# Stores, loads and the start of attention in a hybrid encoder block: three-dimensional query and key stores, whole loads issued early, and a merge that adds in PSUM

## The chip, the core and the metric

The kernel runs on one core of one Trainium2 chip. Its time is the device time of one execution in microseconds (us); three runs of the kernel before took 1420.76, 1419.35 and 1420.70, median 1420.7. TensorE (PE; its weight loads are PEld), VectorE (DVE), ScalarE (ACT), GpSimd (POOL) and SyncE (SP, which only issues DMA here) each run their own instructions in order and wait for each other by semaphores.

## The reference, cut to what matters

One layer of an encoder over 1024 tokens with a width of 1024. Two branches read the same RMS-normalized input through one projection: dilated window attention (three groups of eight heads of 64) and a gated linear recurrence. The part that the change touches is the way of the queries and keys:

```python
for g, (window, dilation) in enumerate(((128, 1), (512, 4), (2048, 16))):
    q = rms_norm(qkv_a[:, :, g, 0], q_norm_w[layer, g])   # over each head's 64 channels
    k = rms_norm(qkv_a[:, :, g, 1], k_norm_w[layer, g])
    v = qkv_a[:, :, g, 2]
    o_g, m_g, d_g = dilated_window_attention(q, k, v, ...)  # keys gathered by residue mod dilation
...
wts = jnp.stack(dens) * jnp.exp(m_all - jnp.max(m_all, axis=0, keepdims=True))
o_a = jnp.sum(wts[..., None] * jnp.stack(outs), axis=0) / jnp.sum(wts, axis=0)[..., None]
y_a = (o_a * silu(g_a)) @ w_proj_a
```

Everything is float32. The kernel splits each operand of a large product into a high and a low part and adds three products.

## The kernel before, in words

**How it is ordered.** A planner in Python (classes Plan and Builder) writes the instructions out once, when the kernel is built. It keeps an estimated time for every engine and every tile. Work is queued as tasks with a priority (a smaller number goes first), the tiles it depends on and, where needed, a condition that a buffer is about to be free. After each few matmuls `tick` issues the tasks whose time by the estimates has come; `burst` does the same for small products on TensorE. `quiet` says whether only weight splits and weight loads are left, and `drain` waits for that. What is issued runs on the chip in that order on each engine, behind semaphores, whatever the real times are. All engine instructions pass through one helper, which is why the profile shows line L60 for all of them; the names of the tiles tell them apart.

**The stages.** The input is normalized and the values are projected (to about 142 us); 27 blocks project queries and keys, gates and others (to 669 us); the products called gp project more columns, with attention between and beside them (to about 845); the three groups are merged (to 915); the recurrence follows (to 1222); then come the output projections (to the end).

**The blocks** (`run_quads`). Each block does seven products out of sums of the input (tiles S0 to S3, each with a high and a low part, 64 KB a partition in all) and of the weights (`qraw`, its differences formed on DVE, its high parts on ACT as `whi`, its low parts on GpSimd or DVE as `wlo`). Twelve of the blocks are queries and keys: group g, side hv (four heads), e (0 for queries, 1 for keys). Each gives two halves of the tokens, and each half has two tiles of 128 partitions, one per value of col, which hold 32 of the 64 channels of each of four heads. They pass through this chain, one task after another: `squares` (ACT, takes two buffers of the ring `ny`, which has four), `sq_sum` (DVE), `sq_high` (ACT), `sq_low` (DVE), `head_sums` (TensorE: two products with ones, tile `nss`), `guess` (ACT, takes three buffers of `ny`), `newton` and `norm_root` (DVE), `scaled` (DVE, once per col), and the store `out` by SP to the DRAM tensor qkD[g, hv, 2e + col], 128 rows (head by head, 32 channels each) of 1024 tokens. There are 48 such stores of 256 KB. Their pieces are 2 KB (group 0, and the keys of group 2), 512 bytes (group 1) or 128 bytes (queries of group 2), because tokens are sorted by residue. A buffer of `ny` is free again when its store has landed.

**Attention's start.** After the blocks, `for pr in range(2)` runs eight gp groups a turn. After the first of them `attention_start` drains the tasks, closes the blocks' pools and that of the sums, opens the rooms for attention and queues the four loads of `h10D` (`back_load`, split by `back_split`; needed before the fifth gp group), and for every (g, hv), beginning with group 2, the loads of keys `ak`, queries `aq`, biases `abias` and eight of values `av`. `load_heads` loads a tile of two heads' halves by four DMAs of 32 partitions with 2 x 4 KB each, since partition 64 j + 32 col + c has to hold channel half col of heads j and 2 + j. The scores (`sc`) are TensorE products of keys and queries, and DVE adds the biases when it reads them.

**The merge.** `merge_maybe` opens the merge's room, and `spread_al` spreads the weights of the three groups over PSUM (three tiles `al`) and has DVE multiply and add: near = al0 x og0, acc = al1 x og1, far = al2 x og2, near + far, acc + near, acc x gate. While it runs, the low parts of the gp weights are made on the engine that `b.low` names: DVE.

Of the kernel before, what the change touches and what calls it, by code (L numbers as in the profile page):

```python
# [9 lines left out]
F32R = mybir.dt.float32r  # L10
# [3 lines left out]
OP = mybir.AluOpType  # L14
# [4 lines left out]
S = 1024  # L19
# [15 lines left out]
VR, PT = 10, 8  # L35
# [200 lines left out]
class Builder:  # L236
# [85 lines left out]
        self.p.t["pe"] = self.p.given  # L322

    def quiet(self):
        return all(t.fn in (self.split_next_page, self.feed) for t in self.tasks)

    def ring(self, pool, tag, bufs, shape, dtype=F32):
        return Ring(self, pool, tag, bufs, shape, dtype)
# [234 lines left out]
class Ring:  # L563
# [30 lines left out]
    def soon(self, n=1):  # L594
        return self.room(n) and self.when(n) <= self.b.p.t["pe"] + self.b.AHEAD
# [60 lines left out]
def hybrid_block(ctx, tc, a, out):  # L656
    b = Builder(ctx, tc, a)
    a_, v_, g_, t_, s_ = b.p.act, b.p.dve, b.p.pool, b.p.pe, b.p.sp
# [15 lines left out]
    hctx = ExitStack()  # L674
# [3 lines left out]
    def bank(name):  # L678
        t = b.bank.get(name=name)
        b.bank.done(t)  # L680
        return t

    stage = b.ring(stg, "stage", 3, [128, 512])
# [71 lines left out]
    hq = [{}, {}]  # L755
    for t in range(2):
        for k in range(2):
            for e in range(2):
                pool = a21pool if (t, k) == (1, 0) else hpool
# [9 lines left out]
    actx = ExitStack()  # L769
# [12 lines left out]
    acc = [v_ring.get() for _ in range(2)]  # L782
# [109 lines left out]
    qkD = dr.tile([3, 2, 4, 128, S], F32, name="qkD")  # L892
# [127 lines left out]
    def root(k):  # L1020
        rs[k] = inv_rms(k, bank("ss"))
        rs["d", k] = spread(rs[k])

    def root_out(k):
        rs["B", k] = spread_out(rs["d", k])
# [20 lines left out]
    at = {0: {11: lambda: root(1)}, 3: {5: lambda: root_out(1), 11: lambda: root(0)}, 7: {5: lambda: root_out(0)}}  # L1046
# [46 lines left out]
    gctx, sctx, tctx = ExitStack(), ExitStack(), ExitStack()  # L1093
    blk = {"n": 0}
# [150 lines left out]
    def scaled(g, hv, e, half, z, y2, o, col, count):  # L1245
        R = RES[g]
        n = 512 // R
        per = lambda t: t.rearrange("p (r u) -> p r u", r=R) if R > 1 else t
        nat = lambda t: t.rearrange("p (u r) -> p r u", r=R) if R > 1 else t
        v_.tensor_tensor(per(o), nat(y2), nat(z), op=OP.mult)  # L1250
        (b.rawr if id(z) in lent else blk["spare"]).done(z)
        count[0] -= 1
        if count[0] == 0:
            blk["y"].done(y2)

        def out():
            to = qkD[g, hv, 2 * e + col]
            if g == 2 and e == 1:
                s_.dma_start(to[:, 512 * half:512 * half + 512], o)
            else:  # L1260
                s_.dma_start(to.rearrange("p (r u) -> p r u", r=R)[:, :, n * half:n * half + n],
                             o.rearrange("p (r u) -> p r u", r=R))
            blk["y"].done(o)
        b.task("sp", [o], out, 1)
# [33 lines left out]

    att = {}

    def attention_start(now=False):
        if att or not (now or (not b.small and b.quiet())):
            return
        b.drain()
        gctx.close()
        sctx.close()
        p = hctx.enter_context(tc.tile_pool(name="h10b", bufs=1, side="right"))
        psum(2)
        b.eager, b.SLACK = True, 0.25
        ap = actx.enter_context(tc.tile_pool(name="attn", bufs=1))  # L1310
        for n, k, shape in (("v", VR, [128, 256]), ("q", 2, [128, 2, S]), ("k", 2, [128, 2, S]),
                            ("s", 6, [128, 3, 4, 64]), ("pt", PT, [128, 2, 2, 128]), ("os", 2, [128, 2, 2, 128]),
                            ("bias", 2, [128, 4, 256])):
            att[n] = b.ring(ap, "a" + n, k, shape)
        for e in range(2):
            hq[e][1, 0] = p.tile([128, 4, 512], F32R, name=f"hb{'hl'[e]}")
        for c in range(4):
            b.task("sp", [], lambda c=c: back_load(c), 1, stage.soon)
        for o, g in enumerate((2, 1, 0)):
            for hv in range(2):  # L1320
                soon = lambda n, k=2 * o + hv: att[n].soon() and (k == 0 or b.wire(3.5))
                for n, f in (("k", load_k), ("q", load_q), ("bias", load_bias)):
                    b.task("sp", [], lambda g=g, hv=hv, f=f: f(g, hv), 2, lambda n=n, soon=soon: soon(n))
                for i in range(8):
                    b.task("sp", [], lambda g=g, hv=hv, i=i: load_v(g, hv, i), 2, lambda soon=soon: soon("v"))

    def back_load(c):
        t = stage.get()
        s_.dma_start(t, h10D[c])
        b.task("act", [t], lambda: back_split(c, t), 2)  # L1330

    def back_split(c, back):
        hi, lo = hq[0][1, 0][:, c], hq[1][1, 0][:, c]
        a_.activation(hi, back, AF.Copy)
        v_.tensor_tensor(lo, back, hi.bitcast(F32), op=OP.subtract)
        stage.done(back)
        att["h"] = att.get("h", 0) + 1

    QT, KT, BIAS, V, left = {}, {}, {}, {}, {"in": 0, "out": 0, "turned": 0}

    def load_heads(t, at):
        for j in range(2):
            for col in range(2):
                s_.dma_start(t[64 * j + 32 * col:64 * j + 32 * col + 32],
                             at[col].rearrange("(p j c) t -> j c p t", p=2, j=2)[j])

    def load_k(g, hv):
        KT[g, hv] = att["k"].get()
        load_heads(KT[g, hv], qkD[g, hv, 2:4])
        score_tasks(g, hv)  # L1350

    def load_q(g, hv):
        QT[g, hv] = att["q"].get()
        load_heads(QT[g, hv], qkD[g, hv, 0:2])
        score_tasks(g, hv)

    def load_v(g, hv, i):
# [239 lines left out]
    def merge_maybe(now=False):  # L1597
        if mer or not (now or len(stored) == 48) or not att:
            return
        if now:  # L1600
            b.drain()
        b.eager, b.SLACK = False, 0.6
        b.low = "dve"
        psum(3)
        actx.close()
        mer["p"] = mctx.enter_context(tc.tile_pool(name="merge", bufs=1, side="right"))
        mer["sel"] = sel = mer["p"].tile([128, 3, 4, 128], F32R, name="sel")
        mer["x"] = mer["p"].tile([128, 8, 128], F32R, name="mx")
        g_.memset(mer["x"].bitcast(F32), 0.0)
        pick = lambda c: ident[:, c:c + 8].rearrange("p (a j) -> p a j", a=4)[:, :, :, None].to_broadcast([128, 4, 2, 64])  # L1610
        for g in range(3):
            v_.tensor_tensor(sel[:, g].rearrange("p a (j c) -> p a j c", j=2), pick(32 * g), pick(32 * g + 8), op=OP.add)
        mer["og"] = b.ring(mer["p"], "og", 6, [128, S])
        mer["gal"] = b.ring(mer["p"], "gal", 2, [128, 512])
        mer["acc"] = b.ring(mer["p"], "macc", 2, [128, 512])
        merge_start()
# [71 lines left out]
    def spread_al(p, half, rows, gate):  # L1688
        al = [bank("al") for _ in range(3)]
        for g in range(3):  # L1690
            t_.matmul(al[g], mer["sel"][:, g, p, :], mer["ab"][:, 512 * half:512 * half + 512], start=True, stop=True)
        nat = lambda t, g: t.rearrange("p (u r) -> p u r", r=(4, 16)[g - 1])

        def per(g):
            U = S // (4, 16)[g - 1]
            return rows[g].rearrange("p (r u) -> p u r", u=U)[:, U // 2 * half:U // 2 * half + U // 2]

        acc, far = mer["acc"].get(), al[2]
        near = rows[0][:, 512 * half:512 * half + 512]
        v_.tensor_tensor(near, al[0], near, op=OP.mult)  # L1700
        v_.tensor_tensor(nat(acc, 1), nat(al[1], 1), per(1), op=OP.mult)
        v_.tensor_tensor(nat(far, 2), nat(al[2], 2), per(2), op=OP.mult)
        v_.tensor_tensor(near, near, far, op=OP.add)
        v_.tensor_tensor(acc, acc, near, op=OP.add)
        v_.tensor_tensor(acc, acc, gate, op=OP.mult)
        b.task("sp", [acc], lambda: (s_.dma_start(oaD[p, half], acc), mer["acc"].done(acc)), 1)
        mer["out"] = mer.get("out", 0) + 1
        mer["gal"].done(gate)
        if half:
            for t in rows.values():  # L1710
                mer["og"].done(t)
# [26 lines left out]
    def evac_qe(h, u):  # L1738
# [4 lines left out]
            store(qD[h, u], t)  # L1743
        return f

    for pr in range(2):
        grs = [tok_group(pos, 128 * i, evac_early(pr, i), last=(i >= 6)) for i in range(8)]
        for k in range(7):
            if pr == 0 and k == 4:
                attention_start(True)  # L1750
                b.until(lambda: att.get("h", 0) == 4)
            b.run_unit(grs[k:k + 1] if k < 6 else grs[6:])
            attention_start()
            merge_maybe()
        pos += 8
# [438 lines left out]
    ep, acc, sgr = ectx["ep"], ectx["acc"], ectx["sg"]  # L2194
# [395 lines left out]
```

## Time and profile before

| | |
|---|---|
| runs | 1420.76, 1419.35, 1420.70 us; median 1420.7 |
| profiled execution | 1421.55 us, its span 1419.8 us (1.75 lies outside the span) |
| mean granted clock of TensorE | 0.997 |
| bytes moved by DMA | 230.29 MB, mean 162 GB/s |
| stores qkD<-ny | 48 of 256 KB, median 3.3 us from issue to landing |
| loads ak<-qkD and aq<-qkD | 24 and 24 of 256 KB, median 6.2 and 8.8 us |

In the rows of the profile, "out<-in" names the tile written and the tiles read, x is the number of instructions, and brackets at the end of a timeline's row say how long the engine had been idle and what released it. In a view by stretches of time the columns are the stretch's length, the busy us of PE, PEld, DVE, ACT and POOL with their numbers of instructions, the granted clock (1.00 is full speed), the share of the 16 DMA engines that was busy, and GB/s. A wait for several things is put down to the one that came last. An issue of a DMA on SP has its start and the time it took SP to issue it; the landing is told separately.

### The profile page before, as it was taken

What the parts mean: (1) busy time and instruction counts of PE and PEld (TensorE: products, weight loads), DVE (VectorE), ACT (ScalarE), POOL (GpSimd) and SP (SyncE); (2) the same over time, 40 slices, a digit from 0 to 9 for tenths busy, and PEclk for the clock granted to TensorE, in tenths of its full rate; (3) what the DMA queues carried; (4) which work ended last, traced back from release to release, by engine and by line L of the source; (5) the groups of instructions that cost most, each with busy time, mean ns of one, the idle gap of its engine ahead of it and who ended that gap; (6) DMA issues with size and microseconds to landing.
All of it is one profiled execution on the core that took longest, in us unless ns stands there. A gap on an engine that the chain in (4) does not pass through costs nothing.

```text
span 1419.8 us, 23915 instructions
## 1 busy us (share of the span) xinstructions
PE 1404.7 (99%) x8506; PEld 1168.3 (82%) x8506; DVE 932.6 (66%) x1889; ACT 840.7 (59%) x1831; POOL 356.6 (25%) x379
## 2 busy tenths in 40 slices
PE   9999999999999999999899999999999999999998
PEld 8788888788888888888778888888888888888887
DVE  6673556776776776331356657887878786358973
ACT  7743554665655646444577553577778784558461
POOL 0101434545433443334032110122222221001011
PEclk9999999999999999999999999999999999999999
DMA  7846568667633344423999429554444452778665
GB/s 238 187 134 188 171 183 190 146 174 172 165 102 99 96 123 136 157 104 126 251 264 261 134 67 318 177 141 124 114 120 120 116 137 73 233 243 218 185 166 137
DMA packets 178915, 230.29 MB, mean 162 GB/s; under 512 B 42227, under 2 KB 102923, under 8 KB 178284
## 3 DMA queue, kind: packets, MB, share of 16 engines
q1 hardware_dynamic: 160988, 193.19, 44.8%
q0 software_dynamic: 16944, 35.40, 13.8%
q8 instruction: 67, 1.10, 0.3%
q14 instruction: 52, 0.43, 0.1%
q10 hardware_dynamic: 864, 0.19, 0.1%
HBM read 168.77 MB, written 81.43 MB: 176 GB/s over the span
## 4 chain that ended last, share of the span: by engine, by line
PE 82%; DVE 7%; DMA 4%; ACT 4%; issue 2%; SPq 0%; POOL 0%; DVEq 0%; ACTq 0%; POOLq 0%
PE gp L60 26%; PE qA L60 18%; PE qE L60 9%; PE sA L60 6%; PE sE L60 5%; PE qC L60 4%; PE u L60 3%; PE oB L60 3%; PE sc L60 2%; PE o L60 2%; DMA qraw<-in_w_in_dram 2%; PE pT L60 1%; DVE ny L60 1%; PE U L60 1%; DMA raw<-in_w_in_dram 1%
## 5 line engine op out<-in xcount | busy, mean ns | idle before, releaser
L60 POOL TENSOR_TENSOR wlo<-qraw,whi 128x512 fp32r<-128x512 f32 x135 | 187.6, 1396 | 375.0 <-ACT whi L60 374.5
L60 ACT ACTIVATE whi<-qraw 128x512 fp32r<-128x512 f32 x189 | 117.8, 626 | 113.8 <-DVE qraw L60 53.1
L60 PE MATMUL gp<-hh,whi 128*128 128x512 f32 x264 | 109.8, 416 | 0.0
L60 DVE TENSOR_TENSOR qraw<-qraw,qraw 128x512 f32<-128x512 f32 x81 | 83.5, 1032 | 34.3 <-DMA qraw<-in_w_in_dram 21.1
L60 PE MATMUL gp<-hh,wlo 128*128 128x512 f32 x264 | 103.8, 393 | 0.0
L60 PE MATMUL gp<-hl,whi 128*128 128x512 f32 x264 | 103.1, 391 | 0.0
L60 ACT ACTIVATE as<-as,neg 128x192 f32<-128x192 f32 (+1 forms) x192 | 77.7, 409 | 25.7 <-DVE neg L60 25.7
L60 PE MATMUL qA<-hh,whi 128*128 128x512 f32 x216 | 84.0, 389 | 0.0
L60 PE MATMUL qA<-hl,whi 128*128 128x512 f32 x216 | 84.0, 389 | 0.0
L60 PE MATMUL qA<-hh,wlo 128*128 128x512 f32 x216 | 84.0, 389 | 0.0
L60 PE MATMUL gp<-whi,hh 128*128 128x512 f32 x192 | 79.6, 414 | 1.0 <-ACT stage L60 1.0
L60 ACT ACTIVATE whi<-raw 128x512 fp32r<-128x512 f32 x92 | 57.3, 626 | 34.4 <-DMA raw<-in_w_in_dram 10.7
L60 POOL COPY mm<-Bc 128x8 f32<-128x8 f32 x64 | 32.6, 539 | 177.7 <-DVE Bc L60 177.7
L60 PE MATMUL gp<-wlo,hh 128*128 128x512 f32 x192 | 75.7, 394 | 0.4 <-DVE wlo L60 0.4
L60 PE MATMUL gp<-whi,hl 128*128 128x512 f32 x192 | 75.5, 393 | 0.0
L60 DVE TENSOR_TENSOR wlo<-qraw,whi 128x512 fp32r<-128x512 f32 x54 | 37.6, 696 | 52.4 <-ACT whi L60 51.4
L60 DVE CUSTOM_DVE_ANT_0 as<-sc,abias 128x192 f32<-128x192 f32 (+1 forms) x192 | 48.6, 308 | 21.6 <-PE sc L60 11.3
L60 POOL DMA_DIRECT2D wlo<-in_w_in_dram x36 | 31.1, 863 | 114.3 <-ACT wlo L60 97.7
L60 PEld LDWEIGHTS gp<-hh,wlo 128*128 128x128 f32 x264 | 49.5, 188 | 11.1
L60 PEld LDWEIGHTS gp<-hh,whi 128*128 128x128 f32 x264 | 49.8, 189 | 8.3
L60 PEld LDWEIGHTS gp<-hl,whi 128*128 128x128 f32 x264 | 49.9, 189 | 8.0
L60 ACT ACTIVATE stage<-gp 128x512 f32<-128x512 f32 x39 | 22.7, 589 | 54.5 <-PE gp L60 43.7
(317 smaller groups left out, 4146.2 us busy)
## 6 DMA issues: line engine op xcount, KB each, us to landing
raw<-in_w_in_dram SPq DMA_DIRECT2D x84, 256.0 KB, 3.6
qraw<-in_w_in_dram SPq DMA_DIRECT2D x60, 256.0 KB, 3.6
qraw<-in_w_in_dram SPq DMA_DIRECT2D x24, 512.0 KB, 4.3
qkD<-ny SPq DMA_DIRECT2D x48, 256.0 KB, 3.3
wlo<-in_w_in_dram POOLq DMA_DIRECT2D x36, 256.0 KB, 4.3
sg<-sgD SPq DMA_DIRECT2D x32, 256.0 KB, 2.9
eraw<-wsD SPq DMA_DIRECT2D x32, 256.0 KB, 3.0
sgD<-stage SPq DMA_DIRECT2D x26, 256.0 KB, 2.2
```

Source lines behind the costliest of these rows:

```text
L60: got = f(*args, **kw)
```

## The change

1. The store of a tile goes to other rows: the 256 rows of queries (or keys) are seen as 4 heads x 2 x 32, and a tile writes 4 x 32 rows at its col. It is still one store, and its pieces have the same size.
2. `load_k` and `load_q` are one DMA each of 128 partitions with 2 x 4 KB (1 MB) instead of four.
3. A new function `attention_room` runs before the first gp group. It closes the sums' pool, opens there (64 KB) the tiles for h10D's parts, the rings of queries, keys and `pt`, and queues the four loads of h10D and the first keys and queries with priority 1.5. `attention_start` keeps the rest. `quiet` passes over tasks of priority 1.5, and the counter of h10D's parts moves to another dictionary.
4. In the merge `b.low` is GpSimd, and `spread_al` writes the second product in place in PSUM, adds it to near, then far, and multiplies near by the gate into acc: six DVE instructions as before.

```diff
     def quiet(self):
-        return all(t.fn in (self.split_next_page, self.feed) for t in self.tasks)
+        return all(t.prio == 1.5 or t.fn in (self.split_next_page, self.feed) for t in self.tasks)
...
         def out():
-            to = qkD[g, hv, 2 * e + col]
+            to = qkD[g, hv].rearrange("a p t -> (a p) t")[256 * e:256 * e + 256].rearrange("(i x c) t -> i x c t", i=4, x=2)[:, col]
             if g == 2 and e == 1:
-                s_.dma_start(to[:, 512 * half:512 * half + 512], o)
+                s_.dma_start(to[:, :, 512 * half:512 * half + 512], o)
             else:
-                s_.dma_start(to.rearrange("p (r u) -> p r u", r=R)[:, :, n * half:n * half + n],
+                s_.dma_start(to.rearrange("i p (r u) -> i p r u", r=R)[:, :, :, n * half:n * half + n],
                              o.rearrange("p (r u) -> p r u", r=R))
...
+    early = {}
+
+    def attention_room():
+        sctx.close()
+        p = hctx.enter_context(tc.tile_pool(name="h10b", bufs=1, side="right"))
+        ap = actx.enter_context(tc.tile_pool(name="attnR", bufs=1, side="right"))
+        for n, k, shape in (("q", 2, [128, 2, S]), ("k", 2, [128, 2, S]), ("pt", PT, [128, 2, 2, 128])):
+            early[n] = b.ring(ap, "a" + n, k, shape)
+        for e in range(2):
+            hq[e][1, 0] = p.tile([128, 4, 512], F32R, name=f"hb{'hl'[e]}")
+        for c in range(4):
+            b.task("sp", [], lambda c=c: back_load(c), 1.5, stage.soon)
+        for f in (load_k, load_q):
+            b.task("sp", [], lambda f=f: f(2, 0), 1.5)
+
     def attention_start(now=False):
...
-        sctx.close()
-        p = hctx.enter_context(tc.tile_pool(name="h10b", bufs=1, side="right"))
...
-        for n, k, shape in (("v", VR, [128, 256]), ("q", 2, [128, 2, S]), ("k", 2, [128, 2, S]),
-                            ("s", 6, [128, 3, 4, 64]), ("pt", PT, [128, 2, 2, 128]), ("os", 2, [128, 2, 2, 128]),
+        att.update(early)
+        for n, k, shape in (("v", VR, [128, 256]), ("s", 6, [128, 3, 4, 64]), ("os", 2, [128, 2, 2, 128]),
                             ("bias", 2, [128, 4, 256])):
...
-                for n, f in (("k", load_k), ("q", load_q), ("bias", load_bias)):
+                for n, f in (("k", load_k), ("q", load_q), ("bias", load_bias))[2 if o == hv == 0 else 0:]:
...
-        b.task("act", [t], lambda: back_split(c, t), 2)
+        b.task("act", [t], lambda: back_split(c, t), 1.5)
...
-    def load_heads(t, at):
-        for j in range(2):
-            for col in range(2):
-                s_.dma_start(t[64 * j + 32 * col:64 * j + 32 * col + 32],
-                             at[col].rearrange("(p j c) t -> j c p t", p=2, j=2)[j])
-
     def load_k(g, hv):
-        KT[g, hv] = att["k"].get()
-        load_heads(KT[g, hv], qkD[g, hv, 2:4])
+        KT[g, hv] = early["k"].get()
+        s_.dma_start(KT[g, hv], qkD[g, hv, 2:4].rearrange("a p t -> p a t"))
         score_tasks(g, hv)
...
-        b.low = "dve"
+        b.low = "pool"
...
-        v_.tensor_tensor(nat(acc, 1), nat(al[1], 1), per(1), op=OP.mult)
+        v_.tensor_tensor(nat(al[1], 1), nat(al[1], 1), per(1), op=OP.mult)
         v_.tensor_tensor(nat(far, 2), nat(al[2], 2), per(2), op=OP.mult)
+        v_.tensor_tensor(near, near, al[1], op=OP.add)
         v_.tensor_tensor(near, near, far, op=OP.add)
-        v_.tensor_tensor(acc, acc, near, op=OP.add)
-        v_.tensor_tensor(acc, acc, gate, op=OP.mult)
+        v_.tensor_tensor(acc, near, gate, op=OP.mult)
...
+    attention_room()
     for pr in range(2):
```

More of the change, by code (lines that the diff above doesn't have):

```diff
@@ L1310, in attention_start @@
         ap = actx.enter_context(tc.tile_pool(name="attn", bufs=1))
-        for n, k, shape in (("v", VR, [128, 256]), ("q", 2, [128, 2, S]), ("k", 2, [128, 2, S]),
-                            ("s", 6, [128, 3, 4, 64]), ("pt", PT, [128, 2, 2, 128]), ("os", 2, [128, 2, 2, 128]),
+        att.update(early)
+        for n, k, shape in (("v", VR, [128, 256]), ("s", 6, [128, 3, 4, 64]), ("os", 2, [128, 2, 2, 128]),
                             ("bias", 2, [128, 4, 256])):
             att[n] = b.ring(ap, "a" + n, k, shape)
[L1315 to L1318, printed above, removed]
         for o, g in enumerate((2, 1, 0)):
@@ L1336, in back_split @@
         stage.done(back)
-        att["h"] = att.get("h", 0) + 1
+        blk["h"] = blk.get("h", 0) + 1
     QT, KT, BIAS, V, left = {}, {}, {}, {}, {"in": 0, "out": 0, "turned": 0}
-    def load_heads(t, at):
-        for j in range(2):
-            for col in range(2):
-                s_.dma_start(t[64 * j + 32 * col:64 * j + 32 * col + 32],
-                             at[col].rearrange("(p j c) t -> j c p t", p=2, j=2)[j])
     def load_k(g, hv):
-        KT[g, hv] = att["k"].get()
-        load_heads(KT[g, hv], qkD[g, hv, 2:4])
+        KT[g, hv] = early["k"].get()
+        s_.dma_start(KT[g, hv], qkD[g, hv, 2:4].rearrange("a p t -> p a t"))
         score_tasks(g, hv)
     def load_q(g, hv):
-        QT[g, hv] = att["q"].get()
-        load_heads(QT[g, hv], qkD[g, hv, 0:2])
+        QT[g, hv] = early["q"].get()
+        s_.dma_start(QT[g, hv], qkD[g, hv, 0:2].rearrange("a p t -> p a t"))
         score_tasks(g, hv)
@@ L1750, in hybrid_block @@
                 attention_start(True)
-                b.until(lambda: att.get("h", 0) == 4)
+                b.until(lambda: blk.get("h", 0) == 4)
             b.run_unit(grs[k:k + 1] if k < 6 else grs[6:])
```

## The prediction

> **What bounds the kernel now.** I read the profile from the top down: busy times, then who TensorE waited for, then the stretches that the change touches, then the chain of waits. The first two views (the page's busy times; TensorE's waits, as total us, times, longest us):
>
> ```profile
> span 1419.8 us, 23915 instructions
> PE 1404.7 (99%) x8506; PEld 1168.3 (82%) x8506; DVE 932.6 (66%) x1889; ACT 840.7 (59%) x1831; POOL 356.6 (25%) x379
> ...
> PE sc L60 <- DMA aq<-qkD: 3.8, 2, 2.2
> ...
> PE nss L60 <- DVE ny L60: 0.4, 1, 0.4
> ```
>
> TensorE sets the time: it is idle for 1419.8 - 1404.7 = 15.1 us of the whole span. Nothing in this change alters a product, so the change can gain only out of these 15.1 us and out of time at a low clock, and it can lose wherever a product comes to wait. The largest wait is for the first queries. The stretches (us of the span; busy us of PE, its weight load, DVE, ACT and POOL, granted clock, DMA share, GB/s):
>
> ```profile
> 205.00:669.00 464.00, 462.75 (x2041) 382.50 (x2040) 290.38 (x338) 259.31 (x450) 192.73 (x153) 1.00 0.50 135
> 682.00:688.00 6.00, 3.81 (x19) 2.87 (x17) 0.09 (x1) 1.88 (x2) 0.63 (x1) 1.00 1.05 217
> 688.00:693.00 5.00, 3.40 (x97) 3.18 (x97) 1.86 (x23) 1.03 (x7) 0.00 (x0) 0.53 1.06 301
> 693.00:700.00 7.00, 7.00 (x29) 5.64 (x29) 4.64 (x35) 5.71 (x28) 0.56 (x1) 0.85 0.97 246
> 700.00:775.00 75.00, 72.09 (x1018) 58.04 (x1016) 42.99 (x268) 57.43 (x246) 23.03 (x27) 1.00 1.00 270
> 850.00:870.00 20.00, 20.00 (x94) 16.30 (x93) 15.30 (x29) 7.57 (x17) 2.39 (x6) 1.00 0.92 307
> ```
>
> Three things are to be seen. The blocks (205 to 669) leave TensorE 464 - 462.75 = 1.25 us of idle time, although their query and key results pass through a long chain on ACT and DVE and back to TensorE (nss). The start of attention has a hole at 682 to 693, and TensorE then runs at a granted clock of 0.53 and 0.85 until 700. And 700 to 775 has 75 - 72.09 = 2.91 us of idle time, beside DMA engines that are full.
>
> **The early loads and the whole loads (gain).** Timelines of TensorE and of SP's queue around the hole, and the landing times of the loads (KB each, median us to landing):
>
> ```profile
> 670.00 0.34 SPq L60 DMA_DIRECT2D gaD<-spare  x1
> ...
> 675.92 0.87 SPq L60 DMA_DIRECT2D stage<-h10D  x2
> 676.96 1.75 SPq L60 DMA_DIRECT2D ak<-qkD  x4
> 678.75 2.28 SPq L60 DMA_DIRECT2D aq<-qkD  x4
> 681.62 1.70 SPq L60 DMA_DIRECT2D abias<-skewD  x2
> ...
> 687.85 0.29 PE L60 MATMUL sc<-ak,aq 64*64 64x64 f32 x2 [2.19 <-DMA aq<-qkD]
> 689.75 0.55 PE L60 MATMUL sc<-ak,aq 64*64 64x64 f32 x9 [1.60 <-DMA aq<-qkD]
> ...
> qkD<-ny SPq DMA_DIRECT2D x48, 256.0 KB, 3.3
> ...
> ak<-qkD SPq DMA_DIRECT2D x24, 256.0 KB, 6.2
> aq<-qkD SPq DMA_DIRECT2D x24, 256.0 KB, 8.8
> og<-oD SPq DMA_DIRECT2D x12, 512.0 KB, 5.2
> ```
>
> Before, eight loads of 32 partitions each are issued from 676.96 on, and the queries are there at 687.85: 2 MB in 10.9 us. Now two loads of 1 MB are queued as soon as the blocks' last sums are read, about 670 by the store of the last block at 670.00, behind three loads of h10D. At the 307 GB/s that whole rows reach in 850 to 870, each takes 1.05 MB / 307 = 3.4 us, the 0.79 MB of h10D's three loads 2.6 us: 670 + 2.6 + 6.8 = 679.4, and with 1 us or so to start and to land, some 7 us earlier. The biases then have none of these eight instructions ahead of them; they are issued near 676 and land, I estimate, as late after it as the keys did (6.2), at about 682. The scores need them only on DVE. So the wait of 3.8 us goes. With it goes the slow clock: 5 x (1 - 0.53) + 7 x (1 - 0.85) = 3.4 us of work that was done late. The five later pairs of loads become two instructions instead of eight, at the rate of og (512 KB in 5.2, against 256 KB in 6.2 and 8.8); I give them half of the 2.91 us of idle time, 1.4. Gain: 3.8 + 3.4 + 1.4 = 8.6 us; bounds 0 (the wait passes to the biases whole) and 3.8 + 3.4 + 2.9 = 10.1.
>
> Moving h10D's loads and the room ahead costs nothing visible: SP is past its last block store, the splits lie on ACT and DVE, which have 1.88 and 0.09 us of work in the 6 us of 682 to 688; without that cover they are four copies and four differences, 0.63 and 0.69 each by the rows of the same size below, 5.3 us.
>
> **The 48 stores (loss).** Their count and bytes stay, but not their shape. The tile's side begins with 128 partitions; the DRAM side began with 128 rows and now begins with four heads, 32 rows inside each. No store of that form is in the trace. Its price is bounded below by 0 (the work is split as before). Above it is bounded by this mechanism: a store is dealt out by its outermost count, so four of the 16 DMA engines carry it, and the transfer takes four times as long. That the shape of a transfer matters at all is in the rows above: 32 partitions at a time took 6.2 to 8.8 for 256 KB, whole rows 5.2 for 512. The Trainium skill, "DMA: Bandwidth & Descriptors", section "Why a DMA increments its semaphore by 16 and not by 1", says that the number of engines is the largest up to 16 that divides the slowest dimension of both sides, which is 4 here; no run here shows it yet, and by it the sum is the one that follows.
>
> I take the upper end, because the outermost count falls below the number of engines, which 32 partitions did not. The 307 GB/s at a share of 0.92 are 334 GB/s for 16 engines, so 262 KB take 0.8 us now and 3.1 us on four: 2.4 us more, and 4.8 for the second of a pair, which queues behind the first on the same four. Who waits (timelines; ACT's waits from 140 to 669; landing of the stores issued from 488 to 512, in pieces of 2 KB, and from 512 to 535, in pieces of 128 bytes):
>
> ```profile
> 215.04 2.94 SPq L60 DMA_DIRECT2D qkD<-ny  x2
> 218.07 2.00 SPq L60 DMA_DIRECT2D qraw<-in_w_in_dram  x2
> ...
> 235.45 0.63 ACT L60 ACTIVATE ny<-raw 128x512 f32<-128x512 f32 x1 [2.38 <-DMA qkD<-ny]
> 236.46 0.63 ACT L60 ACTIVATE ny<-spare 128x512 f32<-128x512 f32 x1 [0.38 <-DMA qkD<-ny]
> 243.34 0.68 DVE L60 TENSOR_TENSOR nlo<-ny,nhi 128x512 fp32r<-128x512 f32 x1
> 245.26 0.39 PE L60 MATMUL nss<-nhi,headones 128*128 128x512 f32 x1
> ...
> 467.37 1.63 SPq L60 DMA_DIRECT2D qkD<-ny  x2
> 470.92 0.63 ACT L60 ACTIVATE ny<-spare 128x512 f32<-128x512 f32 x1 [0.20 <-DMA qkD<-ny]
> 472.63 1.37 DVE L60 TENSOR_TENSOR nlo<-ny,nhi 128x512 fp32r<-128x512 f32 x1 [0.35 <-ACT nhi L60]
> 476.06 0.39 PE L60 MATMUL nss<-nhi,headones 128*128 128x512 f32 x1
> 517.61 9.04 SPq L60 DMA_DIRECT2D qkD<-ny  x2
> ...
> ACT ny L60 <- DMA qkD<-ny: 3.0, 3, 2.4
> ...
> DMA to landing us min/median/max: 2.0/2.0/2.0
> ...
> DMA to landing us min/median/max: 3.5/4.4/5.4
> ```
>
> The four buffers ny hold both the squares of one half of a block and the rows going out of the half before. At 235.45 and 236.46 ACT starts the squares the moment the two stores have landed. From there the chain runs sum, high part, low part (done at 243.34 + 0.68 = 244.0) to the head sums on TensorE at 245.26: only 1.2 us in hand. Squares that start 4.7 us late make TensorE wait 4.7 - 1.2 = 3.5 us (0 to 8, if the load queued at 218.07 behind the pair at 215.04 comes late by as much and holds DVE too). With pieces of 128 bytes the store is dearer: 3.5 against 2.0 to landing, at least, so 1.5 + 0.8 = 2.3 us of transfer, four times that is 9.2, 6.9 more. The pair issued at 467.37 releases ACT at 470.92, and its chain has 476.06 - 474.00 = 2.1 us in hand. If its first store alone is late by 6.9 and a part of the second's delay counts, TensorE waits 5.8 us (0 to 10). The two stores at 517.61 and later are spread over 9 us: 2 us (0 to 7). All other halves together, for whose stores ACT did not wait (the three waits of 3.0 us are the ones at 235.45, 236.46 and 470.92), I put at 1 (0 to 6). Together 12.3 us. Waits of several us also bring back the slow clock, as at 688 to 700: one such, 3.4 us (0 to 10). Loss: 15.7 us, bounds 0 and 41.
>
> The Trainium skill, "TensorE: Matmul & The Clock Gate", Part 1, states that the clock halves after an idle window of about 3.4 us and needs as long of work to return; the rows agree in kind (0.53 after waits of 2.19 and 1.60 us). By it two waits as long as 5.8 us would each cost such a window of half speed, an estimated 3.4 us more in sum than the one that is counted.
>
> **Merge and lows (nothing).** From 845 to 935 (groups: count, busy us, mean ns):
>
> ```profile
> 845.00:915.00 70.00, 70.00 (x332) 57.73 (x323) 53.77 (x87) 26.95 (x47) 4.22 (x8) 1.00 0.72 241
> ...
> L60 DVE TENSOR_TENSOR wlo<-raw,whi 128x512 fp32r<-128x512 f32 x16 | 10.2, 685 | 0.7 <-ACT whi L60 0.7
> L60 DVE TENSOR_TENSOR al<-al,og 128x512 f32<-128x512 f32 x8 | 8.6, 1076 | 0.0
> L60 DVE TENSOR_TENSOR macc<-al,og 128x512 f32<-128x512 f32 x8 | 8.5, 1068 | 0.0
> ...
> L60 POOL TENSOR_TENSOR wlo<-qraw,whi 128x512 fp32r<-128x512 f32 x135 | 187.6, 1396 | 375.0 <-ACT whi L60 374.5
> ```
>
> Sixteen low parts leave DVE (10.2 us) for GpSimd (16 x 1.4 = 22 us, in 90 us of which it works 4 in the first 70). Writing the product back where it lay (al<-al,og 1076) instead of into macc (1068) costs 8 x 8 ns. TensorE is busy for all 70 of 70 us, so there is nothing to gain but a part of the idle time after, and a low part that comes 0.7 us later has a ring of weights ahead of it. 0, bounds -1 and +1; without that lead, 16 x 0.7 = 11 us.
>
> **Sum.** -8.6 + 15.7 + 0 = +7.1 on the profiled execution's own 1421.55 (span 1419.8 and 1.75 around it) = 1428.7. The runs' median, 1420.7, is 0.85 below that execution, so 1428.
>
> **Rivals.** (1) Faster: the stores keep their time, because the split over engines does not follow the outermost count, or because the buffers' leads take the 2.4 us up. Then only the gain stays: 1420.7 - 8.6 = 1412 (1410 to 1416 with its bounds; decided by whether a store lands within 1 us of before). For: ACT waited for these stores three times only, 3.0 us in all, and TensorE for nss 0.4 us. Against: at 235.45 there was nothing in hand. (2) The two cancel: late stores cost TensorE about what the start gains, in one or two halves only (3.5 + 5.8 = 9.3 against 8.6): 1421. For: the wait at 236.46 and the pair at 467 are the tight ones. (3) Worse: the loads queued behind stores on the same four engines are late too, DVE's in-order differences hold back the chain in most blocks, and the first scores wait for the biases instead: gain 3, loss 18, 1436 (to 1445). For: in the chain of waits the load of 218.07 comes right behind a pair. Against: 1.25 us of idle time in 464, weights included, so the weights have a lead and only the head sums feel it.
>
> **How the numbers follow.** Forecast 0.32 (1424 to 1433), rival 1 0.35, rival 2 0.13, rival 3 0.20. The two cases of a loss are one mechanism of two sizes, together 0.52, and within it 1428 is the likelier size, hence the predicted time. The range takes rival 1 and rival 3 in up to the outer tenth: 1411 to 1445. Within 0.2% (2.8 us, about what a measurement of this kernel tells from no change) is rival 2: 0.13; faster 0.35, slower 0.52.
>
> **What would show it.** Right: qkD<-ny lands in over 5 us at the median against 3.3; ACT's squares wait for qkD in many halves; TensorE's waits list nss with several us; the stretch 205 to 669 lengthens by about 12; the wait for aq is gone and the clock at 688 to 700 is 1.0. Wrong: the stores land as before and the blocks end at the same time, which makes it rival 1; a wait for abias at the first scores would void the gain; TensorE idle time at 915 to 935 would void the zero for the merge.

## The result and the profile after

The changed kernel takes 1490.62 us (median; 1485.08 to 1492.06) against 1419.78 us for the kernel before on the same chip: ratio 1.0491, 95% interval 1.0473 to 1.0510, so about 70 us slower. The forecast was 1428 us, with a range of 1411 to 1445.

The page of the changed kernel, first its busy times, then TensorE's waits (total us, times, longest):

```profile
span 1488.6 us, 23869 instructions
PE 1425.2 (96%) x8506; PEld 1177.6 (79%) x8506; DVE 926.2 (62%) x1873; ACT 839.8 (56%) x1831; POOL 378.6 (25%) x395
```

```profile
PE qA L60 <- DVE stage L60: 13.9, 2, 8.8
PE qA L60 <- ACT stage L60: 12.9, 5, 4.7
PE qA L60 <- ACT spare L60: 12.8, 5, 4.7
PE nss L60 <- ACT nhi L60: 6.2, 2, 4.4
PE nss L60 <- DVE ny L60: 2.6, 1, 2.6
PE al L60 <- DVE og L60: 2.0, 3, 1.0
PE nss L60 <- DVE nlo L60: 2.0, 3, 0.9
```

The same 8506 matmuls. The span is 68.8 us longer: 63.4 us of idle TensorE instead of 15.1, so 48.3 us more, and 1425.2 - 1404.7 = 20.5 us more of busy time for the same products. The lower clock accounts for about as much: (1 - 0.984) x 1488.6 - (1 - 0.997) x 1419.8 = 19.6 us by the mean granted clock of each span (0.984 here, 0.997 before). The wait for the first queries is gone from the list; the new waits are in the blocks, and most of them are not at nss but at qA, the blocks' own products, which wait until ACT or DVE has taken an earlier result out of PSUM.

Where the time lies (stretches of the changed kernel: length, busy us of PE, PEld, DVE, ACT, POOL, clock, DMA share, GB/s), and its first scores:

```profile
205.00:645.00 440.00, 389.31 (x1614) 313.00 (x1613) 260.75 (x299) 215.81 (x379) 157.00 (x126) 0.95 0.47 117
645.00:742.00 97.00, 97.00 (x429) 80.33 (x428) 31.27 (x41) 42.36 (x72) 34.95 (x27) 1.00 0.39 128
```

```profile
760.01 1.68 PE L60 MATMUL sc<-ak,aq 64*64 64x64 f32 x96
```

The first scores come at 760.01 instead of 687.85, 72.2 us later; from there to the end of the span it is 1488.6 - 760.0 = 728.6 us instead of 732.0, 3.4 us less. So all of the loss is ahead of attention, spread over the part of the blocks in which queries and keys are stored (205 to 645: 50.7 us idle, clock 0.95). When the last such block is through, TensorE is busy for 97 of 97 us. DMA is not full there (share 0.47).

One such place, the same pair of stores that the prediction looked at. ACT's and TensorE's timelines of the changed kernel:

```profile
233.70 0.63 ACT L60 ACTIVATE whi<-qraw 128x512 fp32r<-128x512 f32 x1 [8.22 <-DVE qraw L60]
...
235.23 0.59 ACT L60 ACTIVATE stage<-qA 128x512 f32<-128x512 f32 x1
...
244.93 0.63 ACT L60 ACTIVATE ny<-raw 128x512 f32<-128x512 f32 x1 [4.76 <-DMA qkD<-ny]
249.07 0.63 ACT L60 ACTIVATE ny<-spare 128x512 f32<-128x512 f32 x1 [3.51 <-DMA qkD<-ny]
```

```profile
235.87 0.50 PE L60 MATMUL qA<-S2h,whi 128*128 128x512 f32 x1 [3.85 <-ACT stage L60]
...
237.67 0.63 PE L60 MATMUL qA<-S2h,whi 128*128 128x512 f32 x1
...
251.08 0.80 PE L60 MATMUL qA<-hh,whi 128*128 128x512 f32 x1 [5.13 <-DVE stage L60]
```

and what came before, from the chain of waits of the changed kernel:

```profile
221.60 11.28 DMA qraw<-in_w_in_dram
232.97 0.70 DVE qraw L60
...
238.57 10.48 DMA qkD<-ny
```

The same load and the same store in the chain of the kernel before:

```profile
218.07 7.69 DMA qraw<-in_w_in_dram
...
231.47 4.97 DMA qkD<-ny
```

ACT waits for both stores of the pair, so their landings show: 249.07 - 244.93 = 4.1 us apart, where they were 236.46 - 235.45 = 1.0 apart before. And a weight load issued at 221.60, right behind the pair of stores before, takes 11.28 us to land, where it took 7.69. DVE stands still for it, ACT behind DVE, and the copy stage<-qA, for which TensorE waits at 235.87, stands behind that on ACT. TensorE's products then take 0.63 us instead of the 0.39 of the full clock.

### The profile page after: what moved, and what is told of

Its sections match the earlier page's. It is cut to its first block, busy times and chain, and to the rows that moved or that the text cites. A ratio compares the mean times of both kernels' runs of the same rounds, so it can differ in the third digit from the quotient of the medians.

```text
span 1488.6 us, 23869 instructions
## 1 busy us (share of the span) xinstructions
PE 1425.2 (96%) x8506; PEld 1177.6 (79%) x8506; DVE 926.2 (62%) x1873; ACT 839.8 (56%) x1831; POOL 378.6 (25%) x395
## 4 chain that ended last, share of the span: by engine, by line
PE 66%; DMA 13%; DVE 10%; ACT 7%; issue 3%; SPq 1%; POOL 0%; DVEq 0%; ACTq 0%; POOLq 0%
PE gp L60 29%; PE qA L60 7%; PE sA L60 6%; DMA qraw<-in_w_in_dram 6%; DMA qkD<-ny 5%; DVE ny L60 4%; PE sE L60 4%; PE qE L60 3%; PE u L60 3%; PE oB L60 3%; PE sc L60 2%; DVE qraw L60 2%; ACT ny L60 2%; ACT whi L60 2%; PE o L60 2%
## 5 line engine op out<-in xcount | busy, mean ns | idle before, releaser
L60 DVE TENSOR_TENSOR qraw<-qraw,qraw 128x512 f32<-128x512 f32 x81 | 78.4, 969 | 87.1 <-DMA qraw<-in_w_in_dram 77.6
L60 PE MATMUL qA<-hh,whi 128*128 128x512 f32 x216 | 87.0, 403 | 14.1 <-DVE stage L60 13.9
L60 PE MATMUL qA<-S2h,whi 128*128 128x512 f32 x108 | 47.8, 442 | 25.8 <-ACT stage L60 12.9
L60 PEld LDWEIGHTS qA<-hh,whi 128*128 128x128 f32 x216 | 42.1, 195 | 24.8 <-DVE stage L60 15.2
L60 POOL TENSOR_TENSOR wlo<-raw,whi 128x512 fp32r<-128x512 f32 x33 | 42.7, 1295 | 61.1 <-ACT whi L60 51.3
```

Source lines behind the costliest of these rows:

```text
L60: got = f(*args, **kw)
```

## The experiments

Each ran beside the kernel before on its chip; ratios are to that.

**Only the outermost count.** The changed kernel with rows interleaved (channel 2c + col of a head instead of 32 col + c, for queries and keys alike, so the scores are the same sums in another order):

```diff
-.rearrange("(i x c) t -> i x c t", i=4, x=2)[:, col]
+.rearrange("(p x) t -> p x t", x=2)[:, col]      # 128 outermost, step of two rows
```

> The changed kernel with one edit: the 256 rows of queries (or keys) are seen as 128 x 2 instead of 4 x 2 x 32, so a tile writes every second row. Count, bytes, pieces, whole loads, early start and merge stay; only the outermost count of the store's DRAM side goes from 4 to 128 (the order of channels inside a head changes alike for queries and keys). Theory A (a store is dealt out by its outermost count, so four DMA engines carried it): the blocks end near 669 us again and the whole is the time before less the gains after the blocks, 1414 to 1417 us. Rival B (stores to rows that lie apart are slow as such, whatever the outermost count): stays slow, 1460 to 1490. Rival C (the blocks are slow for another reason than the stores): 1485 to 1490.

Measured: 1415.70 us, ratio 0.9961 (0.9945 to 0.9976). Against the changed kernel that is 0.053 of the time, 75 us, for the order of two dimensions, with the same stores, bytes and pieces. No two rows of a tile adjoin any more (before this edit 32 did), and the kernel is the faster one, so rival B falls, and C with it. The blocks' idle time is gone; this kernel's stretch and its landings (ACT's timeline):

```profile
205.00:668.00 463.00, 462.84 (x2041) 382.55 (x2040) 289.29 (x338) 259.29 (x450) 192.85 (x153) 1.00 0.51 135
```

```profile
234.25 0.63 ACT L60 ACTIVATE ny<-raw 128x512 f32<-128x512 f32 x1 [1.47 <-DMA qkD<-ny]
235.66 0.63 ACT L60 ACTIVATE ny<-spare 128x512 f32<-128x512 f32 x1 [0.78 <-DMA qkD<-ny]
```

**Eight instead of four.** The changed kernel with

```diff
-.rearrange("(i x c) t -> i x c t", i=4, x=2)[:, col]
+.rearrange("(i x c) t -> i x c t", i=8, x=2)[:, col]
```

> The changed kernel with the rows seen as 8 x 2 x 16 instead of 4 x 2 x 32: outermost count 8. Theory A: eight engines carry a store, its transfer takes twice the 0.8 us of 16 engines instead of four times; the loss in the blocks falls by more than the third that a straight line in transfer time gives (0.8 us more against 2.4: 24 of 73 us), since slack takes up the first microseconds: 0 to 24 us, so 1415 to 1440 us. Rivals B and C: 1485 to 1490.

Measured: 1431.87 us, ratio 1.0075 (1.0058 to 1.0092): 0.0114 or 16 us above interleaved, within what theory A gave. ACT's timeline of this kernel:

```profile
235.27 0.63 ACT L60 ACTIVATE ny<-raw 128x512 f32<-128x512 f32 x1 [2.34 <-DMA qkD<-ny]
237.83 0.63 ACT L60 ACTIVATE ny<-spare 128x512 f32<-128x512 f32 x1 [1.93 <-DMA qkD<-ny]
```

The same pair lands 1.4 us apart with 128 outermost, 2.6 with eight and 4.1 with four, and the loss is 0, 16 and 75 us. I read this as slack that takes up most of the first microsecond and not the next ones.

**The parts by themselves.** First the stores and loads alone, in the kernel before:

```diff
-            to = qkD[g, hv, 2 * e + col]
+            to = qkD[g, hv].rearrange(...)  # four heads, and one 1 MB load a tile
```

> The kernel before with the stores to four heads' rows and the whole loads, and neither the early start nor the merge's edits. Theory A: the whole loss of the blocks, 73 us, less what whole loads bring at the start of attention (0 to 5): 1488 to 1494 us. Rival C: about 1420.

Measured: 1485.98 us, ratio 1.0468 (1.0442 to 1.0493). The loss is all there, a little below the 1488 to 1494 expected.

Then the other two parts, the changed kernel with the stores and loads of before:

```diff
-            to = qkD[g, hv].rearrange(...)     # and whole loads
+            to = qkD[g, hv, 2 * e + col]       # and load_heads
```

> The changed kernel with the stores and the loads of before (48 stores to 128 adjoining rows, four loads of 32 partitions a tile), so only the early start and the merge's edits are left. Theory A: blocks as before, 1413 to 1418 us; the difference to the interleaved kernel is what whole loads bring, 0 to 3 us. Rival C: 1480 or more, since the stores are not what is slow.

Measured: 1421.40 us, ratio 1.0005 (0.9992 to 1.0017): the blocks are as before, but the gain of 3 us or more that was expected isn't there. The early start did what it should at its place (no wait for aq), and in the profiled execution the hole came back later. That execution took 1425.79 us, the longest of ten and 4.4 above their median, so the size of the later hole is not that of a typical run. TensorE's waits, then the stretch after 700, of this kernel:

```profile
PE gp L60 <- ACT stage L60: 3.1, 2, 2.0
...
PE sc L60 <- DMA av<-vD: 1.7, 1, 1.7
```

```profile
700.00:775.00 75.00, 69.25 (x930) 55.54 (x932) 39.42 (x225) 50.79 (x210) 22.15 (x26) 0.95 0.95 250
```

75 - 69.25 = 5.75 us idle at a clock of 0.95, where it was 2.91 at 1.00. With the early start and whole loads (interleaved) the stretch is busy for 73.79 us at 1.00, with a DMA share of 0.81:

```profile
700.00:775.00 75.00, 73.79 (x1033) 60.41 (x1034) 47.02 (x273) 56.59 (x232) 22.85 (x27) 1.00 0.81 266
```

**Whole loads alone.** The kernel before with interleaved rows and the 1 MB loads:

```diff
+            to = ...rearrange("(p x) t -> p x t", x=2)[:, col]
-        load_heads(KT[g, hv], qkD[g, hv, 2:4])
+        s_.dma_start(KT[g, hv], qkD[g, hv, 2:4].rearrange("a p t -> p a t"))
```

> The kernel before with interleaved rows and whole loads, without the early start and the merge's edits. The early start with the narrow loads brought nothing (its hole moved from the keys and queries at 682 to 693 to the values at 700 to 775). Theory (the narrow loads fill the DMA engines, and the whole loads are what brings the gain): 1414 to 1417 us. Rival (both are needed): 1418 to 1421.

Measured: 1415.10 us, ratio 0.9952 (0.9935 to 0.9970), the same as interleaved with all the rest. So the whole loads, with the interleaved rows that they need, bring the gain without the early start, though the first hole is still in this kernel's trace. The interleaved rows by themselves were not timed, but their place is the blocks, and there TensorE is idle for 1.79 us of 205 to 669 in this kernel, no less than the 1.25 before. Its stretches:

```profile
682.00:688.00 6.00, 3.80 (x17) 2.81 (x15) 0.00 (x0) 1.02 (x1) 0.63 (x1) 1.00 0.97 333
688.00:693.00 5.00, 4.53 (x103) 4.17 (x104) 3.06 (x37) 2.30 (x14) 0.00 (x0) 0.66 0.69 196
...
700.00:775.00 75.00, 73.58 (x1019) 59.75 (x1018) 43.83 (x267) 59.50 (x254) 23.05 (x27) 1.00 0.83 279
```

The landings, before and with whole loads (KB each, median us):

```profile
av<-vD SPq DMA_DIRECT2D x48, 128.0 KB, 5.5
```

```profile
ak<-qkD SPq DMA_DIRECT2D x6, 1024.0 KB, 6.3
aq<-qkD SPq DMA_DIRECT2D x6, 1024.0 KB, 8.8
...
av<-vD SPq DMA_DIRECT2D x48, 128.0 KB, 3.7
```

One load of 1 MB lands after a median of 6.3 (ak) and 8.8 us (aq). That is no sooner than before: 6.2 and 8.8 are the medians of four 256 KB loads issued in a row, which move 1 MB together (ak 3.0 to 7.7 us, against 5.0 to 7.1 for the whole one). The values behind them come 1.8 us sooner, but they come nearly as soon (3.9) with narrow loads and the early start, which gained nothing. How the whole loads gain their 7 us is therefore open.

**The merge.** The kernel before with the merge's edits alone:

```diff
-        b.low = "dve"
+        b.low = "pool"
-        v_.tensor_tensor(nat(acc, 1), nat(al[1], 1), per(1), op=OP.mult)
+        v_.tensor_tensor(nat(al[1], 1), nat(al[1], 1), per(1), op=OP.mult)   # and its sums
```

> The kernel before with the merge's edits alone (low parts on GpSimd; the second product written in place in PSUM). In the interleaved kernel TensorE waits 2.0 us in three waits for DVE in the merge (al <- DVE og), which the kernel before does not have. Theory (the PSUM tile al1 is now held through one more DVE instruction, so the next spreading product waits): slower by 1 to 3 us, 1421 to 1424. Rival (the waits only move work, as the prediction had it): within 1 us of before.

And the interleaved kernel with both lines of that diff turned back, or only the second:

> The interleaved kernel with both of the merge's edits undone (sums in SBUF, low parts on DVE). If the held PSUM tile costs what TensorE waits, 2 us faster than interleaved: 1413 to 1414 us, and faster than both kernels. Rival: 1415 to 1416.

> The interleaved kernel with only the place of the additions undone (second product and sum in SBUF), low parts still on GpSimd. If the held PSUM tile is the cause: 1413 to 1414 us, as with both edits undone. If the low parts on GpSimd are: 1415 to 1416.

Measured: ratios 1.0002 (0.9988 to 1.0017), 0.9967 (0.9952 to 0.9982) and 0.9977 (0.9963 to 0.9990), in us 1421.12, 1417.31 and 1417.41. No version differs from its neighbour by more than the intervals leave open, and the merge's edits alone change nothing that could be measured (the upper end, 1.0017, is 2.4 us). The three waits "al <- DVE og" of 2.0 us in the list above are real, but the interleaved kernel with the old merge has them too (TensorE's waits):

```profile
PE al L60 <- DVE og L60: 2.9, 2, 2.2
```

The kernel before with the merge's edits alone has none of them. The waits do not follow the edit, so my theory of the held PSUM tile falls, by them more than by the times.

**One side of six.** The interleaved kernel with four heads' rows for group 0, side 0 alone (8 of 48 stores):

```diff
+            if (g, hv) == (0, 0):
+                far = ...rearrange("(i x c) t -> i x c t", i=4, x=2)[:, col]
+                s_.dma_start(far[:, :, 512 * half:512 * half + 512], o)
```

> The interleaved kernel where only the first of the six sides (group 0, side 0: 8 of the 48 stores, pieces of 2 KB) is stored to four heads' rows. By the changed kernel's loss of 75 us spread evenly over the stores: 8/48 x 75 = 12.5 us more than interleaved, 1427 to 1430 us. By the prediction's list, in which the halves other than three groups cost 1 us together and the wait at 235 is 3.5: at most 5 us more, 1416 to 1421.

Measured: 1429.07 us, ratio 1.0051 (1.0033 to 1.0069): 0.0090 or 13 us more than interleaved, as an even spread gives (12.5), and more than the 5 us at most of the prediction's list.

**By which way the lateness reaches TensorE.** The stores issued by ACT (other DMA queue than the weight loads); six buffers in ny instead of four, paid for by five in spare; and a control of that with interleaved rows:

```diff
-                s_.dma_start(to..., o)         # b.task("sp", [o], out, 1)
+                a_.dma_start(to..., o)         # b.task("act", [o], out, 1)
```

```diff
-        blk["y"] = b.ring(p, "ny", 4, [128, 512])     # SPARE = 7
+        blk["y"] = b.ring(p, "ny", 6, [128, 512])     # SPARE = 5
```

> The changed kernel (four heads outermost) with the 48 stores issued by ACT instead of SP, so that the weight loads of the blocks no longer stand behind them in SP's queue; the buffers of ny still come free only when a store has landed, and ACT pays the issue (48 times about 0.5 us). Theory Q (most of the 73 us comes from loads queued behind the stores on the same DMA engines; the late load holds DVE, then ACT, then TensorE): the loss falls to 35 us at most, under 1455 us, and DVE's waits for qraw loads fall from 77.6 us toward the 21.1 of before. Theory F (most comes from the four buffers of ny, free late): stays above 1465 us with ACT waiting for qkD as in the changed kernel (34.9 us).

> The changed kernel with six buffers in the ring ny instead of four (the room comes from spare, five instead of seven). Theory Q: still over 1460 us. Theory F: under 1440 us, ACT no longer waits for qkD.

> Control for the kernel with six buffers: the same rings with interleaved rows. If the smaller spare ring costs nothing, 1415 to 1418 us as with interleaved rows alone; what it takes more is to be taken off the other.

Measured: 1495.24 us (1.0518; 1.0492 to 1.0545), 1478.87 (1.0385; 1.0351 to 1.0419), control 1422.47 (1.0005; 0.9993 to 1.0018). The control's rings (six in ny, five in spare) cost 0.0044 or 6 us; against that control six buffers leave 0.0380 or 54 us of the 75. The rows that the theories named did move. Waits from 140 to 745, of the kernel before, of the changed kernel, of the stores on ACT's queue, and of six buffers:

```profile
DVE qraw L60 <- DMA qraw<-in_w_in_dram: 21.1, 9, 4.1
```

```profile
ACT ny L60 <- DMA qkD<-ny: 34.9, 12, 5.8
...
DVE qraw L60 <- DMA qraw<-in_w_in_dram: 77.6, 16, 11.3
```

```profile
ACT ny L60 <- DMA qkD<-ny: 53.8, 16, 7.7
...
DVE qraw L60 <- DMA qraw<-in_w_in_dram: 35.6, 9, 7.6
```

```profile
DVE qraw L60 <- DMA qraw<-in_w_in_dram: 90.8, 19, 7.6
```

On its own queue DVE's waits for weights are halved and ACT's for buffers grow; with six buffers ACT's waits are gone and DVE's grow. Each theory's way is there. The buffers alone are not the loss, since 54 us stay without their waits. What the loads alone are worth the first run can't tell, because ACT's waits for buffers grew in it. So both diffs at once, and as a control for ACT's issues the first diff with interleaved rows:

> The changed kernel with both ways closed: stores issued by ACT, six buffers in ny (spare has five). If the two ways are the whole loss: near the control with six buffers plus what ACT's issues cost, under 1445 us, with ACT's waits for qkD and DVE's waits for qraw loads both near those of before. If the stores hold the four engines whoever issues them (the two queues share them): 1460 to 1480 us, with DVE's waits for qraw loads well above 21 us.

> The interleaved kernel with its stores issued by ACT. Control: if issuing from ACT costs nothing much, 1415 to 1420 us; if ACT's issues and the waits in front of them hold its queue up, 1425 to 1440, and that much of the 1495 us of the four-head stores on ACT's queue is not the stores' transfer.

Measured: 1473.00 us (1.0380; 1.0355 to 1.0405) and 1420.61 (1.0002; 0.9993 to 1.0012). Issuing from ACT costs 0.0041 or 6 us by itself, so on ACT's queue alone the four heads cost 0.0516 or 73 us, no less than on SP's. With both diffs DVE waits 27.7 us for loads, near the 21.1 of before but above the 11.4 of the interleaved control on ACT's queue, so that way is narrower and not quite closed. ACT waits only once for a store (5.3 us), and still 1.0380 - 0.9961 - 0.0044 - 0.0041 = 0.0334 or 47 us of loss stand, if the two controls add. The time is the one expected for stores that hold the same four engines whoever issues them, but the sign named for it, DVE's waits well above 21 us, is hardly there. A third way is in ACT's timeline and waits of this kernel:

```profile
469.62 0.52 ACTq L60 DMA_DIRECT2D qkD<-ny  x1
...
471.25 5.91 ACTq L60 DMA_DIRECT2D qkD<-ny  x1
477.20 0.60 ACT L60 ACTIVATE spare<-qA 128x512 f32<-128x512 f32 x1 [6.33 <-issue]
```

```profile
ACT spare L60 <- issue: 23.6, 6, 6.3
...
ACT whi L60 <- issue: 14.2, 5, 5.4
```

The second store of a pair holds the issuing engine for 5.91 us, instead of 0.52. No row names what it waits for; I take it to be the store ahead. Here the engine held is ACT itself, and the copy out of PSUM is 6.33 us late; 23.6 + 14.2 = 37.8 us of ACT stand under "issue" in these two rows, 2.0 in the interleaved control. So the diff that moves the stores to ACT brings a hold of ACT with it, and the 47 us are no measure of what is left in the changed kernel. There it is SP that is held, and everything that SP issues after. Its queue (a row of x2 runs from the start of its first issue to the end of its last):

```profile
503.27 6.09 SPq L60 DMA_DIRECT2D qkD<-ny  x2
509.45 6.83 SPq L60 DMA_DIRECT2D qraw<-in_w_in_dram  x3
525.14 6.13 SPq L60 DMA_DIRECT2D qkD<-ny  x2
```

The pair that is at 525.14 here took SP 1.63 us before (at 467.37). Over all 48 (ns, least, median, most), of the kernel before and of the changed one:

```profile
L60 SPq DMA_DIRECT2D qkD<-ny x48: 319/448/603, 176.1 to 568.9; - x48
```

```profile
L60 SPq DMA_DIRECT2D qkD<-ny x48: 511/528/5097, 176.3 to 642.1; - x48
```

The median moved little: four of the 48 stores held SP for more than 1.5 us, and none of the first 16, those of group 0 with pieces of 2 KB (0.97 us at most). Weight loads behind them were held too, up to 5.9 us for one issue against 2.4 before. The eight stores of one side, which cost 13 us, held SP for 0.93 us at most, so there the first two ways seem to be enough. This third way was read from traces; no run closed it, so how the 75 us divide among the three stays open.

The fastest kernels of the study are interleaved rows with the whole change (1415.70) and whole loads alone (1415.10), both faster than before by 0.4 to 0.5% and not told apart.

## Why the prediction was right or wrong

**The bound and the place: right.** TensorE had 15 us to win, and what the change cost came as TensorE waiting in the blocks. The sign was right, and rivals 1 and 2 are out. Two of rival 3's three ways (loads late behind the stores, DVE's differences held) are what was seen, at four times its size; its third, first scores that wait for the biases, is not among TensorE's waits.

**The mechanism of the stores: right.** The outermost count of 4 is the cause, by the one edit that takes 75 us away. The Trainium skill, "DMA: Bandwidth & Descriptors", section "Why a DMA increments its semaphore by 16 and not by 1", gives the number of engines as the largest up to 16 that divides the slowest dimensions of both sides; by that 16, 8 and 4 engines, and the landings 1.4, 2.6 and 4.1 us apart agree. No view here shows the single engines, so the count of four itself is inferred.

**The price of one store: too low.** Put at 3.1 us of transfer; the pair's landings are 4.1 apart (the estimate took the rate of 4 engines as a quarter of 334 GB/s; 262 KB in 4.1 us are 64 GB/s, a fifth).

**The step that failed is the sum over the halves**: "All other halves together ... I put at 1 (0 to 6)", and with it the 12.3 and the 15.7, whose upper bound was 41. Eight stores of one side alone cost 13 us, and 48 cost 75: 1.6 us a store on average in both. Three reasons, the first two shown by rows, the third from traces only. The prediction looked for lateness at one door, the buffers of ny, and took a half that did not wait for a store before as safe; but slack that hides a landing 1 us late does not hide 4 (the dose of 16 and 75 us). It followed the lateness to nss, with 1.2 us in hand, while TensorE's waits shown above are 39.6 us at qA and 10.8 at nss: a late load holds DVE and ACT, which run in order and also empty PSUM. The load's delay was in the text as a bound of 8 us at one place, against the pair at 215.04; it happened all along the blocks (16 waits of DVE, 77.6 us, against 9 and 21.1). And issues that hold SP were not thought of at all.

**The slow clock: mis-sized with it.** 3.4 us for one wait; measured 20.5 us of extra busy time, beside the eighteen waits of up to 8.8 us at qA and nss. The Trainium skill, "TensorE: Matmul & The Clock Gate", Part 1, has the clock halve after an idle window of about 3.4 us; the trace agrees in kind (0.63 us a product some 2 us after a wait of 3.85).

**The gain at attention's start: total near, split wrong.** 8.6 us forecast; 5.5 (0.0039) measured with the stores mended, 3.4 behind the first scores in the changed kernel. But 7.2 of it were given to the early start and 1.4 to whole loads. The early start alone gave nothing; in its trace the wait moved from the queries to the values, beside DMA engines that the narrow loads kept full (share 0.95). The whole loads with interleaved rows alone gave 0.0048, 7 us. So the hole of 3.8 us named by the waits was not to be bought by starting sooner alone; that full DMA engines made it is my reading and no run shows it. The prediction also took 6.2 and 8.8 us for the price of one narrow load, where they are what a row of four takes.

**Merge and lows: right within the interval.** Nothing, 1.0002 (0.9988 to 1.0017).

## What to carry to other kernels

Look at the outermost dimension of both sides of every DMA. Here, with the same bytes, a count of 8 cost 16 us and a count of 4 cost 75, by later landings of the stores and of the loads behind them, and by an issuing engine that was held. A permutation of channels that both factors of a product share (here queries and keys) can give the wanted rows with 128 outermost, as it did here. And when a stage's slack is small compared with a new delay, price each occurrence, not only those that wait already: in this kernel DVE and ACT work in order and also empty PSUM, and late inputs came out as 39.6 us of TensorE's waits at qA.

## What the runs showed of the hardware

- A store with four rows of heads outermost can hold the engine that issues it right behind another: 5.91 us on ACT and up to 5.1 us on SP for one instruction that took 0.32 to 0.60 before. On SP it was four of the 48 that took more than 1.5 us, and on neither engine one of the first 16, with pieces of 2 KB.
- With stores on ACT's queue and loads on SP's, the loads were less late (35.6 us of DVE's waits against 77.6) but the stores landed later: the same pair 5.0 us apart instead of 4.1 (ACT's timeline of that kernel):

```profile
246.47 0.63 ACT L60 ACTIVATE ny<-raw 128x512 f32<-128x512 f32 x1 [7.38 <-DMA qkD<-ny]
251.47 0.63 ACT L60 ACTIVATE ny<-spare 128x512 f32<-128x512 f32 x1 [4.36 <-DMA qkD<-ny]
```

- Four loads of 32 partitions by 8 KB, issued in a row, landed 3.0 to 7.7 us after their issue (ak, median 6.2); one load of 128 partitions by 8 KB, the same 1 MB, after 5.0 to 7.1 (median 6.3).
